# Four of eight gate/up pairs by sevens, and residual additions and wide h tiles 150 places later in the order

## The chip, the cores and the metric

One NeuronCore of a Trainium2 chip runs the whole program. The time is device microseconds of one execution; the median of 3 runs stands for the kernel. TensorE (PE) multiplies, VectorE (DVE) and ScalarE (ACT) do the elementwise work, SyncE (SP) issues the loads.

## The reference

Two decoder layers over 256 tokens of width 2048, in float32. Layer 0 mixes tokens by causal pooling over four groups, layer 1 by differential attention with ALiBi; each is followed by a SwiGLU network with 5632 hidden columns. RMSNorm stands before each part and at the end.

```python
def swiglu(h, wg, wu, wd):
    return (jax.nn.silu(h @ wg) * (h @ wu)) @ wd

for i in range(DEPTH):
    hn = rmsnorm(h, norm_mix[i])
    mix = pool_mixer(...) if i % 2 == 0 else diff_attention(...)
    h = h + mix
    h = h + swiglu(rmsnorm(h, norm_ffn[i]), w_gate[i], w_up[i], w_down[i])
return rmsnorm(h, final_norm)
```

## The kernel before

**Products in halves.** Every float32 operand is split into a rounded part `hi` and a remainder `lo`, and a product is three matmuls: hi·hi, hi·lo and lo·hi, added up in PSUM.

**A step.** `group` (L138) makes a product of the 256 tokens with 1024 weight columns, in steps of 256 rows of the weight. One step loads one megabyte into `raw` (L107, three buffers), as four blocks of 128 x 512: two row blocks times two column blocks. So a step is a product of 2 x 2 blocks, and it is made in one of two ways:

- *plain*: eight block products into four banks, 24 matmuls. DVE and ACT make `whi` and `wlo` of all four blocks (L112).
- *by sevens*: a scheme of Strassen and Winograd with seven block products, 21 matmuls, into seven banks. Three of them take the raw blocks (A11·B11, A12·B21, S4·B22), four take sums of blocks. DVE makes these sums in `tsum` (L119), and their halves go to `thi` and `tlo` (L127); `whi` and `wlo` are then made of three blocks only. The left operand needs four sums too; they are made once, when the activations are transposed (`pair`, L245, the tile `e`, L260 to L268).

`whi` and `wlo` have three buffers each, `tsum`, `thi` and `tlo` one each.

**Banks.** The eight PSUM banks are named at L135: M1, M6, M7, P5, P3, P4, M2, X = 0 to 7. Plain steps write M2, P3, P4 and X, the others M1, M2, M6, M7, P5, P3, P4. When a group is done, `combined` (L195) adds the banks up into four tiles of 512 columns: two copies on ACT and eight additions on DVE (L202 to L211). The first products of the next group are issued while this goes on, each as soon as its bank is free.

**Gate and up.** `ffn` (L443) has eleven chunks of 512 gate and 512 up columns per layer, in sections of 4, 4 and 3. Each chunk is one group of eight steps (pairs 0 to 7 of the normalised input), of which pairs 2, 4 and 6 go by sevens; in chunk 0 of layer 0 only pair 6 does. After `combined`, ACT makes silu and DVE the product with up (L463, L464), and PE transposes the result into two `h` tiles (L468). Of a section's h tiles, those at places 2, 4 and 6 are made wide (eight blocks, by `e`), since the down product takes these steps by sevens.

**Down.** After each section come two groups over its h tiles, one for each half of the 2048 columns. Their results are added to the residual `x_tok` (L487).

**Order.** The kernel is written as a program in sequence; a scheduler gives each engine a fixed order from priorities that fall in the order of writing, so that work of the next chunk moves up while an engine would wait. `tc.high_priority(-n)` lets what is written in it count as n places later.

**Other places that the change touches.** The pool stage at the start takes its banks at L335. `transposed` (L270) fills the eight `xp` tiles of the next part. In attention, `oT[h]` (L609) holds the heads' results for the output product.

Of the kernel before, what the change touches and what calls it, by code (L numbers as in the profile page):

```python
# [39 lines left out]
SEVEN = (2, 4, 6)  # L40
SEVEN_DOWN = (2, 4, 6)
SEVEN_QKV = (4, 6)
SEVEN_O = (6,)

# [8 lines left out]
def trunk_kernel(ctx, tc, x_n, gains, scale_in, final_in, subln, lam_in, band, dist,  # L53
# [31 lines left out]
    dist_sb = const.tile([P, 2 * P], F32, name="dist_sb")  # L85
    ident = const.tile([P, P], F32, name="ident")
    ones = const.tile([P, P], F32, name="ones")
    nc.vector.memset(ones, 1.0)
    make_identity(nc, ident)

# [47 lines left out]
    def group(steps, pool, by_bank=0):  # L138
# [14 lines left out]
        ps = {}  # L153
# [9 lines left out]
        def products(a, seven, w, b, parts):  # L163
            first = b not in ps
            if first:
                ps[b] = bank(b)
            for at, which, block in parts:
                hi, lo = w[which]
                if seven:
                    ah, al = a[:, 0, at], a[:, 1, at]  # L170
                else:
                    k, t = at
                    if a.shape[2] == 8:
                        slot = ((A11, A21), (A12, A22))[k][t]
                        ah, al = a[:, 0, slot], a[:, 1, slot]
                    else:
                        ah, al = (a[:, k, i, t * P:(t + 1) * P] for i in range(2))
                for x, y in ((ah, hi), (ah, lo), (al, hi)):
                    left[b] -= 1
                    nc.tensor.matmul(ps[b], x, y[:, block], start=first, stop=(left[b] == 0))  # L180
                    first = False
# [13 lines left out]
    def combined(ps, pool):  # L195
# [4 lines left out]
        m1, u2, u3, p5 = (pool.tile([P, 512], F32, name=f"c{i}") for i in ("11", "12", "21", "22"))  # L200
# [5 lines left out]
        nc.vector.tensor_tensor(u2, p5, u2, ALU.subtract)  # L206
        nc.vector.tensor_tensor(p5, p5, u3, ALU.subtract)
        nc.vector.tensor_tensor(u2, ps[P3], u2, ALU.add)
        nc.vector.tensor_tensor(u3, ps[P4], u3, ALU.add)
# [35 lines left out]
    def pair(dst, src, gains, seven):  # L245

        ps = aux((P, 2, 2, P))
# [14 lines left out]
        for i, at in ((0, slice(A21, A11 + 1)), (1, slice(A22, A12 + 1, A12 - A22))):  # L262
            nc.scalar.activation(e[:, at], ps[:, i], AF.Copy, scale=1.0 if gains is None else gains[i])
        nc.vector.tensor_tensor(e[:, S1:S3 + 1], e[:, A21:A11 + 1], e[:, A22:A21 + 1], ALU.subtract)
        nc.vector.tensor_tensor(e[:, S2], e[:, S1], e[:, A11], ALU.subtract)
        nc.vector.tensor_tensor(e[:, S4], e[:, A12], e[:, S2], ALU.add)
        nc.scalar.copy(dst[:, 0], e)
        nc.vector.tensor_tensor(dst[:, 1], e, f32(dst[:, 0]), ALU.subtract)  # L268
# [11 lines left out]
    with tc.tile_pool(name="start", bufs=1, reuse_waits="tile") as st:  # L280

        warm = tmp.tile([P, 8], F32, name="warm", bufs=1)
        nc.scalar.activation(warm[:, 0:1], ones[:, 0:1], AF.Sqrt)
# [159 lines left out]
    def ffn(layer, xq, ss, next_op, next_gain):  # L443
# [62 lines left out]
    with tc.tile_pool(name="attn", bufs=1, reuse_waits="tile") as ap_, ExitStack() as heads:  # L506
# [4 lines left out]
            small[:, a:b] for a, b in ((0, 2), (2, 4), (4, 8), (8, 10), (10, 12), (12, 13), (14, 16)))  # L511
        nc.sync.dma_start(out=subln_sb, in_=subln)
# [3 lines left out]

        nc.vector.tensor_tensor(lp, lam_sb[:, 0:2], lam_sb[:, 2:4], ALU.mult)
# [75 lines left out]
        for g in range(2):  # L593
            cs = scaled(combined(group([(xp[p], p in SEVEN_QKV, w_v[g, p]) for p in range(NP)], op_), op_), (r_col, r_col))
            for h in range(4 * g, 4 * g + 4):
# [13 lines left out]
                oT[h] = op_.tile(pair_shape(h in SEVEN_O), F32R, name=f"oT{h}")  # L609
# [99 lines left out]
```

## Time and profile before

| | |
|---|---|
| median of 3 runs | 1845.67 us (1845.63 to 1845.70) |
| the profiled execution | 1846.21 us, its span 1844.4 us |
| granted TensorE clock | 0.997 |
| gate/up chunk, from its predecessor's transposes to its own (1267.02 to 1309.80) | 42.78 us |
| whole FFN of layer 1, first gate/up section (1184 to 1351): PE, DVE, ACT busy | 167.00, 151.15, 92.34 of 167 us |
| same layer, first down section (1351 to 1435): PE, DVE, ACT busy | 84.00, 76.19, 42.72 of 84 us |

Lines of the profile are lines of the kernel; most matmuls have line 180, that of the helper in `group`, and are told apart by their tiles. PEld is the load of the stationary operand, which overlaps the matmuls. Busy times of one engine count overlapping instructions once; the mean of a group is the length of one instruction. "Idle before" is the time in which an engine stood still ahead of an instruction, with what released it.

### The profile page before, as it was taken

To read this page: it belongs to the slowest core of one execution; us is meant where nothing else is said; L and a number is where in the kernel's file an instruction comes from. 1 tells how busy PE (TensorE), PEld (TensorE's weight loads), DVE (VectorE), ACT (ScalarE), POOL (GpSimd) and SP (SyncE) were. 2 spreads that over 40 slices of the span, in tenths; PEclk is the share of its full clock that TensorE was granted. 3 is DMA by queue.
4 is the path that set the end of the run, shared out by engine and by line. 5 is a ranking of instruction groups with operands and counts; after the bars stand their busy time and mean duration, and the time that the engine had idled before them with its cause. 6 is when DMAs were issued, how large, how long until landed. Compare 5 with 4: busy or idle time off the path is not lost.

```text
span 1844.4 us, 20901 instructions
## 1 busy us (share of the span) xinstructions
PE 1829.2 (99%) x8210; PEld 1495.6 (81%) x8210; DVE 1604.2 (87%) x1662; ACT 1038.0 (56%) x1006; POOL 0.7 (0%) x6
## 2 busy tenths in 40 slices
PE   9999999999999999999999999999999999999998
PEld 6788888888888888888888888788888888888886
DVE  6889998898989899988888678998989899998986
ACT  6555555555554556665566655555555555545553
POOL 0000000000000000000000000000000000000000
PEclk9999999999999999999999999999999999999999
DMA  7555555655555555555454454555555555565552
GB/s 273 183 201 187 193 210 194 210 196 194 203 198 204 202 186 183 208 180 171 173 177 164 160 188 176 205 203 187 204 205 204 188 201 183 206 227 204 206 186 111
DMA packets 50642, 356.80 MB, mean 193 GB/s; under 512 B 6000, under 2 KB 6128, under 8 KB 8048
## 3 DMA queue, kind: packets, MB, share of 16 engines
q1 hardware_dynamic: 49824, 353.85, 54.4%
q10 hardware_dynamic: 720, 1.62, 0.2%
q8 instruction: 64, 1.05, 0.2%
q14 instruction: 34, 0.28, 0.0%
HBM read 353.36 MB, written 2.10 MB: 193 GB/s over the span
## 4 chain that ended last, share of the span: by engine, by line
PE 95%; DVE 2%; ACT 1%; issue 1%; DMA 1%; SPq 0%; DVEq 0%; ACTq 0%
PE b L180 90%; PE b L250 2%; PE b L342 1%; DVE wlo L116 1%; PE b L554 1%; PE b L345 1%; PE b L584 0%; DMA w<-pool_w 0%; DMA raw<-w_gu 0%; DVE tlo L131 0%; ACT whi L115 0%; DVE tsum L121 0%; PE b L600 0%; PE b L598 0%; PE b L599 0%
## 5 line engine op out<-in xcount | busy, mean ns | idle before, releaser
L115 ACT CAST whi<-raw 128x1536 fp32r<-128x1536 f32 (+1 forms) x330 | 585.2, 1774 | 585.4 <-PE b L180 499.6
L180 PE MATMUL b<-whi,xp 128*128 128x512 f32 x2824 | 908.8, 392 | 1.2 <-DVE c L203 1.0
L116 DVE TENSOR_TENSOR wlo<-raw,whi 128x1536 fp32r<-128x1536 f32 (+1 forms) x330 | 697.3, 2113 | 193.1 <-ACT whi L115 192.9
L180 PEld LDWEIGHTS b<-whi,xp 128*128 128x128 f32 x2824 | 528.3, 188 | 110.1 <-DVE c L203 1.5
L180 PE MATMUL b<-wlo,xp 128*128 128x512 f32 x1412 | 551.8, 391 | 1.6 <-DVE wlo L116 1.6
L180 PE MATMUL b<-whi,h 128*128 128x512 f32 x1108 | 354.5, 390 | 0.0
L180 PEld LDWEIGHTS b<-wlo,xp 128*128 128x128 f32 x1412 | 265.3, 188 | 55.5 <-DVE wlo L116 1.9
L131 DVE TENSOR_TENSOR tlo<-tsum,thi 128x2048 fp32r<-128x2048 f32 x108 | 246.7, 2285 | 3.9 <-ACT thi L130 3.9
L180 PEld LDWEIGHTS b<-whi,h 128*128 128x128 f32 x1108 | 207.5, 188 | 43.1
L180 PE MATMUL b<-wlo,h 128*128 128x512 f32 x554 | 215.8, 389 | 0.0
L130 ACT CAST thi<-tsum 128x2048 fp32r<-128x2048 f32 x108 | 206.3, 1910 | 13.7 <-DVE tsum L124 13.6
L180 PE MATMUL b<-thi,xp 128*128 128x512 f32 x608 | 211.8, 390 | 0.0
L121 DVE TENSOR_TENSOR tsum<-raw 128x1024 f32<-128x1024 f32 x108 | 131.8, 1220 | 2.3 <-DMA raw<-w_v 0.6
L180 PEld LDWEIGHTS b<-thi,xp 128*128 128x128 f32 x608 | 113.9, 188 | 24.0 <-ACT thi L130 0.9
L180 PEld LDWEIGHTS b<-wlo,h 128*128 128x128 f32 x554 | 104.0, 188 | 21.3
L180 PE MATMUL b<-tlo,xp 128*128 128x512 f32 x304 | 119.5, 393 | 0.0
L180 PE MATMUL b<-thi,h 128*128 128x512 f32 x240 | 83.7, 389 | 0.0
L124 DVE TENSOR_TENSOR tsum<-tsum,raw 128x512 f32<-128x512 f32 x108 | 74.3, 688 | 2.3
L123 DVE TENSOR_TENSOR tsum<-tsum,raw 128x512 f32<-128x512 f32 x108 | 73.9, 684 | 0.6
L180 PE MATMUL b<-whi,oT 128*128 128x512 f32 x236 | 74.4, 392 | 0.0
L180 PEld LDWEIGHTS b<-tlo,xp 128*128 128x128 f32 x304 | 57.0, 188 | 16.1 <-DVE tlo L131 4.4
L180 PEld LDWEIGHTS b<-thi,h 128*128 128x128 f32 x240 | 45.1, 188 | 9.2
(147 smaller groups left out, 1192.5 us busy)
## 6 DMA issues: line engine op xcount, KB each, us to landing
raw<-w_gu SPq DMA_DIRECT2D x176, 1024.0 KB, 4.9
raw<-w_down SPq DMA_DIRECT2D x88, 1024.0 KB, 4.8
raw<-w_qk SPq DMA_DIRECT2D x32, 1024.0 KB, 4.9
raw<-w_v SPq DMA_DIRECT2D x16, 1024.0 KB, 4.8
raw<-w_o SPq DMA_DIRECT2D x16, 1024.0 KB, 4.8
raw<-pool_w SPq DMA_DIRECT2D x2, 1024.0 KB, 13.8
x_tok<-x_n SPq DMA_DIRECT2D x2, 768.0 KB, 9.0
w<-pool_w SPq DMA_DIRECT2D x2, 512.0 KB, 6.6
```

Of the source, the lines that this page charges most:

```text
L115: nc.scalar.copy(hi[:, lo_block:], raw[:, lo_block:])
L116: nc.vector.tensor_tensor(lo[:, lo_block:], raw[:, lo_block:], f32(hi[:, lo_block:]), ALU.subtract)
L121: nc.vector.tensor_tensor(t[:, T1:T3 + 1], raw[:, B11:B22 + 1], raw[:, B12:B12 + 1].broadcast_to([P, 2, 512]), ALU.add)
L123: nc.vector.tensor_tensor(t[:, T2], t[:, T1], raw[:, B22], ALU.add)
L124: nc.vector.tensor_tensor(t[:, T4], t[:, T2], raw[:, B21], ALU.add)
L130: nc.scalar.copy(hi, t)
L131: nc.vector.tensor_tensor(lo, t, f32(hi), ALU.subtract)
L180: nc.tensor.matmul(ps[b], x, y[:, block], start=first, stop=(left[b] == 0))
L250: nc.tensor.transpose(ps[:, i, 1 - t if seven else t], src(i, t), ident)
L342: nc.tensor.matmul(yp[g][t], a[:, rows], w[:, at], start=(at == 0), stop=(at == 3))
L345: nc.tensor.matmul(yp[g][t], u, v[:, at], start=(at == 0 and j == 0), stop=(at == 3 and j == 2))
L554: nc.tensor.matmul(sc[:, :nk], qk[:, 0, c, qb * P:(qb + 1) * P], qk[:, 1, c, :nk], start=True, stop=True)
```

## The change

Pair 0 joins the pairs that go by sevens in gate/up, in all chunks except the first of each layer. The first chunk of layer 0 keeps pair 6 alone, that of layer 1 pairs 2, 4 and 6.

The order of the seven products changes: in a group's first step M1, M2, P5, M7, M6, P3, P4, in later ones M1, M2, P3, P5, M7, M6, P4. P3 and P4 become one tile of two banks, and the four results of `combined` one tile `c`, so that four of its additions become two of double width. The transposes of the h tiles go to bank X instead of taking turns in banks 0 to 3.

The additions to the residual (except in a layer's last section) become two of 1024 columns and are put back by 150 places; so are the sums and halves of the wide h tiles. To make room, `dist_sb`, `ones`, `part` and `oT[4..7]` get other places.

```diff
-SEVEN = (2, 4, 6)
+SEVEN = (0, 2, 4, 6)
+BEHIND = 150
...
+    def two_banks():
+        both = psum.tile([P, 2, 512], F32, name="b45", tag="b45")
+        return [both[:, i] for i in range(2)], both
...
+    def behind(n):
+        return tc.high_priority(-n) if n else nullcontext()
...
             if seven:
-                plan.append([(M1, [(A11, 0, B11)]), (M2, [(A12, 0, B21)]), (M6, [(S2, 1, T2)]), (M7, [(S3, 1, T3)]),
-                             (P5, [(S1, 1, T1)]), (P3, [(S4, 0, B22)]), (P4, [(A22, 1, T4)])])
+                raw = [(M1, [(A11, 0, B11)]), (M2, [(A12, 0, B21)]), (P3, [(S4, 0, B22)])]
+                summed = [(P5, [(S1, 1, T1)]), (M7, [(S3, 1, T3)]), (M6, [(S2, 1, T2)]), (P4, [(A22, 1, T4)])]
+                late = 3 if plan else 2
+                plan.append(raw[:late] + summed[:3] + raw[late:] + summed[3:])
...
-            first = b not in ps
-            if first:
+            first = b not in opened
+            opened.add(b)
+            if first and b in (P3, P4) and b not in ps:
+                (ps[P3], ps[P4]), ps["both"] = two_banks()
+            elif first and b not in ps:
                 ps[b] = bank(b)
...
-        m1, u2, u3, p5 = (pool.tile([P, 512], F32, name=f"c{i}") for i in ("11", "12", "21", "22"))
+        c = latest["c"] = pool.tile([P, 4, 512], F32, name="c")
+        m1, u2, u3, p5 = (c[:, i] for i in range(4))
...
-        nc.vector.tensor_tensor(u2, p5, u2, ALU.subtract)
-        nc.vector.tensor_tensor(p5, p5, u3, ALU.subtract)
-        nc.vector.tensor_tensor(u2, ps[P3], u2, ALU.add)
-        nc.vector.tensor_tensor(u3, ps[P4], u3, ALU.add)
+        nc.vector.tensor_tensor(c[:, 1:4:2], c[:, 3:4].broadcast_to([P, 2, 512]), c[:, 1:3], ALU.subtract)
+        nc.vector.tensor_tensor(c[:, 1:3], ps["both"], c[:, 1:3], ALU.add)
...
-        ps = aux((P, 2, 2, P))
+        ps = aux((P, 2, 2, P)) if at is None else bank(at, (P, 2, 2, P))
...
+        with behind(BEHIND if at is not None else 0):
+            nc.vector.tensor_tensor(e[:, S1:S3 + 1], e[:, A21:A11 + 1], e[:, A22:A21 + 1], ALU.subtract)
+            nc.vector.tensor_tensor(e[:, S2], e[:, S1], e[:, A11], ALU.subtract)
+            nc.vector.tensor_tensor(e[:, S4], e[:, A12], e[:, S2], ALU.add)
+            nc.scalar.copy(dst[:, 0], e)
+            nc.vector.tensor_tensor(dst[:, 1], e, f32(dst[:, 0]), ALU.subtract)
...
-                    by_seven = SEVEN[-1:] if g == 0 and layer == 0 else SEVEN
+                    by_seven = SEVEN if g else SEVEN[1:] if layer else SEVEN[-1:]
...
-                        pair(ht, lambda k, t: cs[t][1][:, (2 * i + k) * P:(2 * i + k + 1) * P], None, at in SEVEN_DOWN)
+                        pair(ht, lambda k, t: cs[t][1][:, (2 * i + k) * P:(2 * i + k + 1) * P], None, at in SEVEN_DOWN, X)
...
+                    if not last:
+                        with behind(BEHIND):
+                            for t in range(2):
+                                to = x_tok[:, t, o * 1024:(o + 1) * 1024]
+                                nc.vector.tensor_tensor(to, latest["c"][:, 2 * t:2 * t + 2].rearrange("p b n -> p (b n)"),
+                                                        to, ALU.add)
+                        continue
...
+        dist_sb = hq.tile([P, 2 * P], F32, name="dist_sb")
+        nc.sync.dma_start(out=dist_sb, in_=dist)
...
+                if h < 4:
+                    oT[h] = op_.tile(pair_shape(h in SEVEN_O), F32R, name=f"oT{h}")
+                else:
+                    oT[h] = resid.tile(pair_shape(h in SEVEN_O), F32R, name="xp", tag=f"xp{h}")
```

More of the change, by code (lines that the diff above doesn't have):

```diff
@@ L1 @@
 import math
-from contextlib import ExitStack
+from contextlib import ExitStack, nullcontext
 import concourse.bass as bass
@@ L73, in trunk_kernel @@
     turn = {"aux": 0, "of": 4}
+    latest = {}
     def bank(i, shape=(P, 512)):
         return psum.tile(list(shape), F32, name=f"b{i}", tag=f"b{i}")
+    def two_banks():
+        both = psum.tile([P, 2, 512], F32, name="b45", tag="b45")
+        return [both[:, i] for i in range(2)], both
     def aux(shape=(P, 512)):
@@ L84, in trunk_kernel @@
     gain_sb = const.tile([P, 6, NK], F32, name="gain_sb")
-    dist_sb = const.tile([P, 2 * P], F32, name="dist_sb")
     ident = const.tile([P, P], F32, name="ident")
-    ones = const.tile([P, P], F32, name="ones")
-    nc.vector.memset(ones, 1.0)
-    make_identity(nc, ident)
     x_tok = resid.tile([P, 2, D], F32, name="x_tok")
@@ L152, in group @@
                 left[b] = left.get(b, 0) + 3 * len(parts)
-        ps = {}
+        ps, opened = {}, set()
         def prepared(seven, src):
@@ L243, in split, with pair @@
         nc.vector.scalar_tensor_tensor(dst[:, 1, :], src, gain, f32(dst[:, 0, :]), ALU.mult, ALU.subtract)
-    def pair(dst, src, gains, seven):
-        ps = aux((P, 2, 2, P))
+    def pair(dst, src, gains, seven, at=None):
+        ps = aux((P, 2, 2, P)) if at is None else bank(at, (P, 2, 2, P))
         for i in range(2):
@@ L260, in pair @@
         e = tmp.tile([P, 8, P], F32, name="e", bufs=1)
[L262 to L268, printed above, removed]
+        for i, to in ((0, slice(A21, A11 + 1)), (1, slice(A22, A12 + 1, A12 - A22))):
+            nc.scalar.activation(e[:, to], ps[:, i], AF.Copy, scale=1.0 if gains is None else gains[i])
+        with behind(BEHIND if at is not None else 0):
[4 more added lines that the diff above has]
+            nc.vector.tensor_tensor(dst[:, 1], e, f32(dst[:, 0]), ALU.subtract)
     def transposed(xp, j, gain, seven=()):
@@ L280, in trunk_kernel @@
     with tc.tile_pool(name="start", bufs=1, reuse_waits="tile") as st:
+        ones = st.tile([P, P], F32, name="ones")
+        nc.vector.memset(ones, 1.0)
         warm = tmp.tile([P, 8], F32, name="warm", bufs=1)
+        make_identity(nc, ident)
         nc.scalar.activation(warm[:, 0:1], ones[:, 0:1], AF.Sqrt)
@@ L334, in product @@
             if some[0] == 0:
-                yp[g] = [bank(4 + 2 * (g % 2) + t) for t in range(2)]
+                yp[g] = [bank(6 + t) for t in range(2)] if g % 2 else two_banks()[0]
                 if g >= PLAIN:
@@ L413, in trunk_kernel @@
     turn["of"] = 4
-    nc.sync.dma_start(out=dist_sb, in_=dist)
     def finish(cs, ys, final_sb, ss):
         for t in range(2):
-            part = tmp.tile([P, 64], F32, name="part", bufs=2)
+            part = tmp.tile([P, 8], F32, name="warm", bufs=1) if t == 0 else \
+                tmp.tile([P, 2, 4], F32, name="ss").rearrange("p a b -> p (a b)")
             nc.vector.tensor_reduce(part[:, 0:1], ss[:, t, 0:2], AX.X, ALU.add)
@@ L515, in trunk_kernel @@
         nc.vector.tensor_scalar(qs_col, r_col, QK_SCALE, None, ALU.mult)
+        ones = hq.tile([P, P], F32, name="ones")
+        nc.vector.memset(ones, 1.0)
         nc.vector.tensor_tensor(lp, lam_sb[:, 0:2], lam_sb[:, 2:4], ALU.mult)
@@ L608, in trunk_kernel @@
                     nc.scalar.activation(on[:, t, :], op[:, t, :], AF.Copy, scale=ro[:, t:t + 1])
-                oT[h] = op_.tile(pair_shape(h in SEVEN_O), F32R, name=f"oT{h}")
+                if h < 4:
+                    oT[h] = op_.tile(pair_shape(h in SEVEN_O), F32R, name=f"oT{h}")
+                else:
+                    oT[h] = resid.tile(pair_shape(h in SEVEN_O), F32R, name="xp", tag=f"xp{h}")
                 pair(oT[h], lambda i, t: on[:, t, i * P:(i + 1) * P], [gs[:, i:i + 1] for i in range(2)], h in SEVEN_O)
```

## The prediction

> **What bounds the kernel now.** I read the shares and the chain of waits on the page first, then the page's waits for TensorE's weight loads.
>
> ```profile
> span 1844.4 us, 20901 instructions
> PE 1829.2 (99%) x8210; PEld 1495.6 (81%) x8210; DVE 1604.2 (87%) x1662; ACT 1038.0 (56%) x1006; POOL 0.7 (0%) x6
> PE 95%; DVE 2%; ACT 1%; issue 1%; DMA 1%; SPq 0%; DVEq 0%; ACTq 0%
> PEld b L180 <- DVE tlo L131: 6.9, 17, 0.4
> ```
>
> TensorE (PE) holds 95% of the chain that ended last and nearly all of it is line 180, the weight products. It waits for almost nothing: the longest total on its weight loads is 6.9 us for `tlo`, 17 times. So today a matmul taken out is time taken out. VectorE (DVE) at 87% is the second engine, and it is the one that this change loads. The chain in order of time (start, us, engine, line, count) gives the price of a matmul, and under it two windows of one gate/up chunk each (PE's clock, DMA share and GB/s at the end; asked for DVE alone, so the busy time is DVE's) give the state of DVE:
>
> ```profile
> 1267.02 0.66 PE b L250 x6
> 1267.68 41.44 PE b L180 x181
> 1309.80 0.65 PE b L250 x6
> 1310.45 124.34 PE b L180 x547
> ```
>
> ```profile
> 96.58:138.99 42.41, 37.70 (x34) 1.00 0.57 198
> 1267.02:1309.80 42.78, 38.90 (x37) 1.00 0.56 197
> ```
>
> A run of 547 products takes 124.34 us: 0.2273 us from one to the next (each lasts longer; they overlap). A gate/up chunk, from transposes to transposes, is 1309.80 - 1267.02 = 42.78 us. In it DVE is busy 38.90 us; in the one from 96.58, in which both h tiles made are plain, 37.70. What DVE does with the rest, from the waits of DVE in 1267 to 1309.8, and what ACT waits for in the whole run:
>
> ```profile
> DVE wlo L116 <- ACT whi L115: 3.7, 3, 1.6
> ACT whi L115 <- PE b L180: 499.6, 224, 4.7
> ```
>
> DVE's 3.7 us are waits for ACT's casts, and those wait for PE to give a weight buffer back. So DVE is idle because it is ahead, with all buffers full: a spare of 3.7 us a chunk, and 42.78 - 3.7 = 39.1 us is what its work there occupies.
>
> **The change part by part.**
>
> *Fewer products.* A plain step issues 4 banks x 2 parts x 3 = 24 matmuls, a step by sevens 7 x 3 = 21. SEVEN gains pair 0, but not in chunk 0 of either layer, so 20 of 22 chunks lose 3 matmuls: 60 x 0.2273 = **-13.6 us** on the engine that sets the end; a chunk's need of PE falls from 42.78 to 42.1. The Trainium skill, "TensorE: Matmul & The Clock Gate", section "Part 2: What happens when you issue a matmul", gives about 216 ns between matmuls of 512 columns; this trace has 227. By the page the saving would be 12.9 us, an estimate from its figure; the trace decides.
>
> *More preparation.* Each of these 20 steps gets three sums and a second pair of halves. In order of time on DVE:
>
> ```profile
> 1305.41 0.68 DVE L207 TENSOR_TENSOR c<-c,c 128x512 f32<-128x512 f32 x1
> 1306.01 0.68 DVE L208 TENSOR_TENSOR c<-b,c 128x512 f32<-128x512 f32 x1
> 1306.61 0.68 DVE L209 TENSOR_TENSOR c<-b,c 128x512 f32<-128x512 f32 x1
> 1307.21 0.68 DVE L211 TENSOR_TENSOR c<-b,c 128x512 f32<-128x512 f32 x1
> 1307.81 1.40 DVE L464 SCALAR_TENSOR_TENSOR c<-c,r_tok,c 128x512 f32<-128x512 f32 x2
> ...
> 1311.74 0.68 DVE L255 TENSOR_TENSOR h<-b,h 128x512 fp32r<-128x512 f32 x1
> ...
> 1319.65 1.75 DVE L116 TENSOR_TENSOR wlo<-raw,whi 128x1536 fp32r<-128x1536 f32 x1
> 1321.32 1.22 DVE L121 TENSOR_TENSOR tsum<-raw 128x1024 f32<-128x1024 f32 x1
> 1322.57 0.69 DVE L123 TENSOR_TENSOR tsum<-tsum,raw 128x512 f32<-128x512 f32 x1
> 1323.30 0.69 DVE L124 TENSOR_TENSOR tsum<-tsum,raw 128x512 f32<-128x512 f32 x1
> 1323.91 2.28 DVE L116 TENSOR_TENSOR wlo<-raw,whi 128x2048 fp32r<-128x2048 f32 x1
> 1326.11 2.28 DVE L131 TENSOR_TENSOR tlo<-tsum,thi 128x2048 fp32r<-128x2048 f32 x1
> 1328.43 1.23 DVE L121 TENSOR_TENSOR tsum<-raw 128x1024 f32<-128x1024 f32 x1
> ```
>
> From start to start, `wlo` of three blocks takes 1.67, the sums 1.25, 0.73 and 0.61, `tlo` 2.32: 6.58 us, at best 6.3 where nothing depends on the line before. The plain `wlo` it replaces takes 2.20. So +4.1 to +4.4; I take 4.25 a chunk, 85 us of DVE in all. What ACT adds, from the groups kept apart by shape:
>
> ```profile
> L115 ACT CAST whi<-raw 128x2048 fp32r<-128x2048 f32 x222 | 424.9, 1914 | 375.4 <-PE b L180 342.5 <-ACT h L254 18.4 <-issue 4.6
> L130 ACT CAST thi<-tsum 128x2048 fp32r<-128x2048 f32 x108 | 206.3, 1910 | 13.7 <-DVE tsum L124 13.6
> L115 ACT CAST whi<-raw 128x1536 fp32r<-128x1536 f32 x108 | 160.4, 1485 | 210.0 <-PE b L180 157.1 <-DVE c L209 33.7 <-issue 16.8
> ```
>
> One more cast of 1910 ns and one of 1485 in place of 1914: +1.5 us a chunk. ACT is 56% busy and hides it. DMA moves the same megabyte a step.
>
> The rows also show that one DVE instruction starts 0.60 us after the one before though it lasts 0.68: the ends overlap. The Trainium skill, "VectorE: DVE Perf Modes", section "Terms", says under DRAIN that the next operation cannot issue until the pipe is empty. Read as the recorded length, that would make lengths add up; the trace shows them overlapping by 0.08, so I add starts.
>
> *Merged additions.* In `combined` four DVE operations (L206 to L209) become two of 1024 elements. The nearest row is L121, 1024 elements with a broadcast: 1.13 to 1.25 apart. 4 x 0.60 = 2.40 becomes 2.3 to 2.5: between -0.1 and +0.1 a chunk; if PSUM read across two banks cost twice, +1.1. I take -0.1, as reads from PSUM (L208) and SBUF (L207) last alike. The residual additions, 4 x 0.60 merged into 2 x 1.13, likewise.
>
> *The sum on DVE.* 39.1 + 4.25 - 0.1 = 43.2 us in a chunk with one h tile by sevens, 42.0 where both are plain, against PE's 42.1: the spare of 3.7 turns into a deficit of 1.1. This is the heart of the case. What softens it: gate/up chunks come in runs of four, four and three. The first of a run has plain h tiles (no deficit); the last one's `e` work is put back by 150 places, past most of the 180 products of a chunk, so into the down projection. That work, in lengths and less 0.08 for each overlap, is 0.34 + 0.2 + 0.2 + 1.14 = 1.9 us:
>
> ```profile
> L268 DVE TENSOR_TENSOR h<-e,h 128x1024 fp32r<-128x1024 f32 x16 | 19.5, 1218 | 0.0
> L264 DVE TENSOR_TENSOR e<-e 128x256 f32<-128x256 f32 x25 | 10.4, 417 | 0.6 <-ACT e L263 0.4
> L266 DVE TENSOR_TENSOR e<-e 128x128 f32<-128x128 f32 x25 | 7.0, 282 | 0.0
> L265 DVE TENSOR_TENSOR e<-e 128x128 f32<-128x128 f32 x25 | 7.0, 280 | 0.0
> ```
>
> A run of four then wants 42.0 + 43.2 + 43.2 + 41.3 = 169.7 against 168.4, a run of three 126.5 against 126.3. It begins with DVE about 3 us ahead, and the down groups let it catch up:
>
> ```profile
> 1351.00:1393.00 42.00, 38.08 (x33) 1.00 0.56 201
> ```
>
> There DVE keeps its 3.9 us of idle, as down's sevens do not change. On average the deficit (1.3 us a run) fits into the lead, so it costs nothing by the mean.
>
> *Where it does not fit.* `tsum`, `thi` and `tlo` have one buffer each. `thi` of the next step by sevens can only be cast when the last product of the one before is done; cast 1.9 and `tlo` 2.2 make it ready 4.3 us (with the handover) later, and PE wants it after one plain step and its first raw products, 24 x 0.2273 + 6 x 0.2273 = 6.8 us. So the lead is never over 2.5 to 3 us, and at a chunk's end the same window holds `combined`. Around a boundary DVE now owes, from the end of step 6 to the first use of step 2's sums, 5.5 + 12.3 = 17.8 us: two `tlo` 4.5, `combined` 4 x 0.60 + 2 x 1.15 = 4.7, L464 1.3, L255 0.6, `wlo` 2.2 + 1.67, one set of sums 2.6: 17.6 us. That is even. A handover or two of 0.1 to 0.2 us that does not overlap is a PE stall, between 0 and 0.7 us a chunk. I take 0.2: 20 x 0.2 = **+4 us**.
>
> *Order of the banks, and the put-back.* Later sevens run nine raw products ahead of the sums instead of six, 3 x 0.23 = 0.7 us more time for `tlo`; this can end the waits shown above, each 0.4 of a weight load: bounds 0 and -6.9. I take **-1** as chunks' first step has only six. The residual additions put back (2 x 1.13 us) fall into the next stage's middle: DVE is full there in gate/up, so moving them gains at the boundary what it costs later: 0, bounds -1 and +2. If they ran too late, the cast into the single tile `c` at the next chunk's end would queue behind them on ACT and with it the following `whi` casts; 150 places are about 24 us of a 42 us chunk, so it has some 10 us left.
>
> *Elsewhere.* xp0 by sevens, once per layer, adds an `e` (1.9 us) in place of two splits, 2 x (0.48 - 0.08) = 0.8 us:
>
> ```profile
> L243 DVE SCALAR_TENSOR_TENSOR xp<-b,gain_sb,xp 128x256 fp32r<-128x256 f32 x32 | 14.4, 477 | 0.5 <-ACT xp L242 0.4
> ```
>
> Before the first chunk of layer 0 this may show, 0 to +1; I take 0.5. `dist_sb` loaded later, `ones` twice, oT in the xp buffers: none delays a reader in the rows; 0.
>
> Sum against the profiled execution's own 1846.2 (span 1844.4 and 1.8 around it; the median of the three runs is 1845.7): 1846.2 - 13.6 + 4 - 1 + 0.5 = 1836.1, and half a microsecond less on the median. I say **1836**.
>
> **The rivals.**
>
> *Wholly hidden.* The spare and the order suffice; the 60 products go and half of the `tlo` waits: 1846 - 13.6 - 2 = about 1830.5. For it: DVE's mean in the FFN stays under PE's. Against: 17.6 of 17.8 us at each boundary, with no room for a handover.
>
> *A new wait at bank X eats the gain.* All transposes of a chunk now share bank 7, one pair after the other, and step 1's last six products want it.
>
> ```profile
> 1305.53 0.39 PE L180 MATMUL b<-whi,h 128*128 128x512 f32 x1
> ...
> 1310.16 0.66 ACT L263 ACTIVATE e<-b 128x256 f32<-128x256 f32 x2 [2.10 <-PE b L250]
> ```
>
> The next group's products begin at 1305.53 and L255, the last reader of the transposes, ends at 1312.42: 6.9 us after. One pair after the other adds about 0.5 of transposes and up to 1.3 of reading (0.66 of L263, 0.68 of L255): 7.4 to 8.7. PE wants the bank after (21 + 18) x 0.2273 = 8.9 us. If DVE is 0.9 us late, 0.68 a chunk is lost, all of the saving: 1846.
>
> *DVE becomes the bound (the slower side).* In gate/up DVE's need, 43.2 us, sets the chunk if the lead is not held, from the point where its need passes 42.78, today's chunk. Then 20 x (43.2 - 42.78) = +8.4: 1854. For it: the trace's own sum exceeds PE's need; single buffers. Against: the deferred `e` and plain tiles bring a run's mean to 42.4 and down's 3.9 us lie between the runs.
>
> *Lengths add on DVE.* If each DVE instruction held up the next for its whole length, the chunk's 37 and two more would each take 0.08 us more: 43.2 + 39 x 0.08 = 46.3 a chunk, 20 x (46.3 - 42.78) = +70: 1916. The rows L207 to L211 above speak against it, each starts before the last has ended. (This is what the Trainium skill's DRAIN rule would make of the time.)
>
> **How the numbers follow.** The forecast (1832 to 1842 its own range, stalls of 0 to 0.5 us a chunk): 0.60. Wholly hidden, 1829 to 1832: 0.12. Eaten at bank X or by other waits, 1842 to 1849: 0.13. DVE bound, 1850 to 1860: 0.13. Lengths add: 0.02. About 0.2% (3.7 us) is what a measurement of this kernel can tell from no change. So faster 0.72, same 0.13, slower 0.15. The range 1830 to 1849 leaves out the last two and a little of the second.
>
> **What would show it.** Right: 60 fewer matmuls at L180; gate/up chunks of 42.1 to 42.6 us; DVE's waits for `whi` in them nearly gone; PE's weight loads waiting for `tlo` or `wlo` a few tenths a chunk, first at chunk boundaries, less in the first chunk of a run. Wrong towards slower: chunks of 43 us in a row with DVE never idle. Wrong towards bank X: PE waits that name L255 or L211 just ahead of step 1's end. If the two merged operations last over 1.3 us, my price of `combined` fails.

## The result, and the profile after

The changed kernel takes **1909.26 us** (median of 4 runs, 1907.07 to 1911.53), the kernel before 1845.68 (4 runs, 1845.63 to 1845.84). The ratio is 1.0344, 95% interval 1.0326 to 1.0362: slower by 3.4%, where 1836 was forecast. The profiled execution took 1911.5 us, its span 1909.8.

The page of the changed kernel: the span, the engines' busy time with their instructions, and the chain that ended last by engine.

```profile
span 1909.8 us, 20743 instructions
PE 1850.7 (97%) x8150; PEld 1479.4 (77%) x8150; DVE 1677.5 (88%) x1649; ACT 1055.8 (55%) x1028; POOL 0.7 (0%) x6
PE 76%; DVE 13%; ACT 4%; issue 4%; DMA 3%; SPq 0%; ACTq 0%; DVEq 0%
```

The 60 matmuls are gone (8150 in place of 8210), and still the chain holds 76% of TensorE where it held 95%. DVE took its place in the chain, with 13%, though its share of busy time hardly moved (87% to 88%). At the price that the prediction took for a product, 60 x 0.2273 = 13.6 us were saved, so 63.6 + 13.6 = **77.2 us** of waiting are new: 3.9 us for each of the 20 chunks that the change gives a fourth step by sevens.

The waits of the changed kernel (engine, line and tile that waits, what released it: total us, times, longest), and below them those of the kernel before:

```profile
ACT thi L135 <- DVE tsum L129: 193.4, 66, 5.5
DVE tlo L136 <- ACT thi L135: 79.4, 46, 2.3
PEld b L190 <- DVE tlo L136: 28.6, 40, 2.0
PEld b L190 <- ACT thi L135: 24.6, 50, 1.4
PE b L190 <- DVE tlo L136: 16.9, 18, 1.5
```

```profile
ACT thi L130 <- DVE tsum L124: 13.6, 29, 4.0
DVE tlo L131 <- ACT thi L130: 3.9, 3, 2.0
```

This is one chain, seen at each of its links: DVE makes the sums, ACT's cast waits for them (13.6 us became 193.4), DVE waits for the cast to make `tlo` (3.9 became 79.4), and TensorE waits for both halves (6.9 us before for `tlo`).

Where it happens, from windows of the changed kernel, one chunk of a section of four each (start to end; width, busy us of PE, PEld, DVE, ACT and POOL; clock, DMA share, GB/s). The marks are the starts of `combined`'s last addition, L220:

```profile
360.38:403.00 42.62, 41.09 (x178) 31.86 (x176) 37.76 (x33) 22.93 (x18) 0.00 (x0) 1.00 0.41 150
403.00:451.99 48.99, 46.32 (x199) 36.22 (x200) 46.81 (x40) 26.37 (x21) 0.00 (x0) 1.00 0.59 213
451.99:498.48 46.49, 43.39 (x183) 34.16 (x182) 41.50 (x37) 24.31 (x20) 0.00 (x0) 0.96 0.51 183
498.48:540.00 41.52, 41.52 (x189) 34.19 (x188) 37.52 (x33) 22.54 (x18) 0.00 (x0) 1.00 0.56 203
```

The first three windows are the second to fourth chunk of a section, the last one is the down group behind them, whose steps by sevens did not change; it keeps its 41.5. Against the 42.1 us that TensorE needs, the chunks lose 0.5, 6.9 and 4.4 us (the first of the section, not shown, 3.7): 15.5 in all, or 3.9 a chunk, the mean from above. The single numbers are rough, because the mark does not always fall at the same product (the first three windows hold 178, 199 and 183 instructions of TensorE, the one not shown 193); the sum over the section is not touched by that. The loss of a boundary falls just behind its mark, so into the window that begins there. DVE stands still for 2 to 5 us in each: it is not simply full.

The boundary at 403.00 in order of time, first DVE (start, us, engine, line, tile, idle before it and who ended that):

```profile
389.79 0.69 DVE L129 TENSOR_TENSOR tsum<-tsum,raw 128x512 f32<-128x512 f32 x1
392.53 2.29 DVE L136 TENSOR_TENSOR tlo<-tsum,thi 128x2048 fp32r<-128x2048 f32 x1 [2.06 <-ACT thi L135]
394.74 1.75 DVE L121 TENSOR_TENSOR wlo<-raw,whi 128x1536 fp32r<-128x1536 f32 x1
396.59 0.69 DVE L213 TENSOR_TENSOR c<-b,c 128x512 f32<-128x512 f32 x1
397.20 1.22 DVE L126 TENSOR_TENSOR tsum<-raw 128x1024 f32<-128x1024 f32 x1
398.33 0.69 DVE L214 TENSOR_TENSOR c<-b,c 128x512 f32<-128x512 f32 x1
398.94 0.68 DVE L215 TENSOR_TENSOR c<-b,c 128x512 f32<-128x512 f32 x1
399.53 0.68 DVE L128 TENSOR_TENSOR tsum<-tsum,raw 128x512 f32<-128x512 f32 x1
400.13 1.22 DVE L217 TENSOR_TENSOR c<-c 128x1024 f32<-128x1024 f32 x1
401.27 0.69 DVE L129 TENSOR_TENSOR tsum<-tsum,raw 128x512 f32<-128x512 f32 x1
401.87 1.22 DVE L218 TENSOR_TENSOR c<-b,c 128x1024 f32<-128x1024 f32 x1
403.00 0.68 DVE L220 TENSOR_TENSOR c<-b,c 128x512 f32<-128x512 f32 x1
...
404.28 2.29 DVE L136 TENSOR_TENSOR tlo<-tsum,thi 128x2048 fp32r<-128x2048 f32 x1
```

then ACT and TensorE:

```profile
392.88 1.49 ACT L120 CAST whi<-raw 128x1536 fp32r<-128x1536 f32 x1
...
402.35 1.89 ACT L135 CAST thi<-tsum 128x2048 fp32r<-128x2048 f32 x1
```

```profile
396.63 0.39 PE L190 MATMUL b<-thi,xp 128*128 128x512 f32 x1
...
403.72 0.40 PE L190 MATMUL b<-whi,xp 128*128 128x512 f32 x1
404.30 0.96 PE L190 MATMUL b<-thi,xp 128*128 128x512 f32 x3 [0.18 <-ACT thi L135]
...
406.63 0.50 PE L190 MATMUL b<-tlo,xp 128*128 128x512 f32 x1 [1.02 <-DVE tlo L136]
```

The `tlo` at 392.53 is that of step 6 of the chunk that ends. It is the last reader of `tsum`, and `tsum` has one buffer. So the sums for step 0 of the next chunk, the new ones, cannot begin before 394.82, although DVE stands idle for 2.06 us just before, and that step's weights are there by 392.88, when ACT casts them. From 394.82 on, DVE's fixed order has `wlo` and the first addition of `combined` ahead of them, so they run from 397.20 to 401.96, spread between `combined`'s additions, which free the banks. Then come the cast (402.35) and `tlo` (404.28 to 406.57). TensorE begins the last product of step 6 at 396.63. It has used up step 0's raw products by 403.95 and starts its first `tlo` product at 406.63. In the kernel before, step 0 was plain: between step 6 and step 2 there was time for the chain to go round.

### The profile page after: what moved, and what is told of

The parts are those of the page before. It is cut to its first block, busy times and chain, and to the rows that moved or that the text cites. A ratio compares the mean times of both kernels' runs of the same rounds, so it can differ in the third digit from the quotient of the medians.

```text
span 1909.8 us, 20743 instructions
## 1 busy us (share of the span) xinstructions
PE 1850.7 (97%) x8150; PEld 1479.4 (77%) x8150; DVE 1677.5 (88%) x1649; ACT 1055.8 (55%) x1028; POOL 0.7 (0%) x6
## 4 chain that ended last, share of the span: by engine, by line
PE 76%; DVE 13%; ACT 4%; issue 4%; DMA 3%; SPq 0%; ACTq 0%; DVEq 0%
PE b L190 72%; DVE wlo L121 4%; DMA raw<-w_gu 2%; ACT whi L120 2%; DVE tlo L136 2%; DVE tsum L126 1%; PE b L259 1%; DVE c L217 1%; ACT thi L135 1%; PE b L355 1%; DVE c L218 1%; DVE c L213 1%; DVE c L215 1%; DVE c L214 1%; PE b L578 1%
## 5 line engine op out<-in xcount | busy, mean ns | idle before, releaser
L190 PE MATMUL b<-whi,xp 128*128 128x512 f32 x2732 | 883.2, 393 | 9.6 <-ACT whi L120 4.3
L136 DVE TENSOR_TENSOR tlo<-tsum,thi 128x2048 fp32r<-128x2048 f32 x128 | 292.9, 2288 | 80.4 <-ACT thi L135 79.4
L135 ACT CAST thi<-tsum 128x2048 fp32r<-128x2048 f32 x128 | 244.4, 1910 | 200.1 <-DVE tsum L129 193.4
L190 PE MATMUL b<-thi,xp 128*128 128x512 f32 x784 | 270.1, 402 | 6.7 <-ACT thi L135 6.4
L190 PEld LDWEIGHTS b<-thi,xp 128*128 128x128 f32 x784 | 144.0, 189 | 51.2 <-ACT thi L135 24.6
L190 PE MATMUL b<-tlo,xp 128*128 128x512 f32 x392 | 158.0, 403 | 16.9 <-DVE tlo L136 16.9
L126 DVE TENSOR_TENSOR tsum<-raw 128x1024 f32<-128x1024 f32 x128 | 155.9, 1218 | 2.4 <-DMA raw<-w_v 1.7
L190 PEld LDWEIGHTS b<-tlo,xp 128*128 128x128 f32 x392 | 74.4, 190 | 42.8 <-DVE tlo L136 28.0
L129 DVE TENSOR_TENSOR tsum<-tsum,raw 128x512 f32<-128x512 f32 x128 | 87.7, 685 | 1.2
L128 DVE TENSOR_TENSOR tsum<-tsum,raw 128x512 f32<-128x512 f32 x128 | 87.5, 684 | 0.5
L476 ACT ACTIVATE c<-c,r_tok 128x512 f32<-128x512 f32 x44 | 31.8, 722 | 35.0 <-DVE c L214 20.8
```

The costliest lines, as they stand in the source:

```text
L126: nc.vector.tensor_tensor(t[:, T1:T3 + 1], raw[:, B11:B22 + 1], raw[:, B12:B12 + 1].broadcast_to([P, 2, 512]), ALU.add)
L128: nc.vector.tensor_tensor(t[:, T2], t[:, T1], raw[:, B22], ALU.add)
L129: nc.vector.tensor_tensor(t[:, T4], t[:, T2], raw[:, B21], ALU.add)
L135: nc.scalar.copy(hi, t)
L136: nc.vector.tensor_tensor(lo, t, f32(hi), ALU.subtract)
L476: nc.scalar.activation(gate, gate, AF.Silu, scale=r[:, t:t + 1])
```

## The experiments

The theory to which the runs led: **one buffer of `tsum`** ties step 0's sums to the end of step 6's chain and so into `combined`. It was not the first one: the expectations, written before each run, speak at first of the load of pair 0 and of the round trip through ACT (A), and later of VectorE having too much to do (A1) against a chain laid open at each boundary whatever the load (A2). That the buffer is that of `tsum` was written down only after a second buffer for `thi` had brought little. B is the put-back, C the order or bank X. The rivals: DVE is simply full (capacity); the put-back of 150 places delays what is needed; the new order of the seven products; the transposes in one bank X; the detour through ACT for the cast.

**One part taken back at a time.** First, pair 0 plain again, with all the rest of the change kept:

```diff
-                    by_seven = SEVEN if g else SEVEN[1:] if layer else SEVEN[-1:]
+                    by_seven = SEVEN[1:] if g or layer else SEVEN[-1:]
```

> The changed kernel with pair 0 plain again in every chunk; the order of the banks, the merged additions, bank X and the put-back all stay. Theory A (pair 0's preparation overloads VectorE and lays open its round trip through ScalarE; the rest of the change is about neutral): 1840 to 1850 us, within 5 us of before. Theory B (the put-back by 150 places spoils the order): still over 1880. Theory C (the single bank X or the new bank order makes the waits): still over 1870, with waits of the transposes.

Measured 1847.05 us, ratio 1.0004 (0.9994 to 1.0013). All that is slow lies in the fourth step by sevens; order, merged additions, bank X and put-back together cost nothing that can be told from zero as long as pair 0 is plain. Two of its waits belong beside those above:

```profile
ACT thi L135 <- DVE tsum L129: 86.4, 31, 4.2
DVE tlo L136 <- ACT thi L135: 48.3, 32, 2.1
```

They too are far longer than in the kernel before (13.6 and 3.9 us), and yet no time is lost, because TensorE's weight loads wait only 1.2 us for `thi` and `tlo`. The upper links of the chain can wait without harm; its last link decides.

The put-back taken out:

```diff
-BEHIND = 150
+BEHIND = 0
```

> The changed kernel with nothing put back (0 places instead of 150). Theory A: 1900 to 1925, the put-back moves VectorE work about and does not remove it. Theory B: under 1870. Theory C: as A.

1922.04 us, ratio 1.0411 (1.0390 to 1.0432): 12.8 us slower than the change. The put-back is not at fault; it helps.

The old order of the seven products:

```diff
-                raw = [(M1, [(A11, 0, B11)]), (M2, [(A12, 0, B21)]), (P3, [(S4, 0, B22)])]
-                summed = [(P5, [(S1, 1, T1)]), (M7, [(S3, 1, T3)]), (M6, [(S2, 1, T2)]), (P4, [(A22, 1, T4)])]
-                late = 3 if plan else 2
-                plan.append(raw[:late] + summed[:3] + raw[late:] + summed[3:])
+                plan.append([(M1, [(A11, 0, B11)]), (M2, [(A12, 0, B21)]), (M6, [(S2, 1, T2)]), (M7, [(S3, 1, T3)]),
+                             (P5, [(S1, 1, T1)]), (P3, [(S4, 0, B22)]), (P4, [(A22, 1, T4)])])
```

> The changed kernel with the old order of the seven products (M1, M2, M6, M7, P5, P3, P4). Theory A: the first sum is wanted 0.7 us earlier in later steps, so 1909 to 1930. Theory C, if the order is at fault: under 1880.

1908.97 us, ratio 1.0340 (1.0320 to 1.0361): no difference from the change. The order is no cause.

The two pairs of transposes in two banks:

```diff
-                        pair(ht, lambda k, t: cs[t][1][:, (2 * i + k) * P:(2 * i + k + 1) * P], None, at in SEVEN_DOWN, X)
+                        pair(ht, lambda k, t: cs[t][1][:, (2 * i + k) * P:(2 * i + k + 1) * P], None, at in SEVEN_DOWN, (X, M1)[i])
```

> The changed kernel with the second pair of transposes of each chunk in bank M1 instead of X. Theory A: the waits of the transposes on ScalarE's e and on L477 were 11 us in all, so 1898 to 1912. Theory C, if bank X is at fault: under 1880.

1914.23 us, ratio 1.0369 (1.0348 to 1.0390): 5 us slower than with one bank, and 2 us above what was expected; why was not followed up. The rival of bank X falls.

**Is DVE full?** Pair 0 by sevens only in chunks 4 and 8 of each layer, the first of a section, where the down groups before have let DVE catch up:

```diff
-                    by_seven = SEVEN if g else SEVEN[1:] if layer else SEVEN[-1:]
+                    by_seven = SEVEN if g in (4, 8) else SEVEN[1:] if g or layer else SEVEN[-1:]
```

> The changed kernel with pair 0 by sevens in chunks 4 and 8 of each layer alone, the first of a run, whose h tiles are plain (4 chunks, 12 matmuls fewer, -2.7 us). Theory A1 (the deficit builds up over a run, VectorE has too much to do): 1841 to 1847 us, the spare of the chunks around carries it. Theory A2 (at each boundary into a step by sevens the round trip from the sums through ScalarE's cast back to VectorE is laid open, whatever the load): some 3 us for each of the four, 1850 to 1860.

1858.42 us, ratio 1.0064 (1.0047 to 1.0081), that is 11.4 us over the version with pair 0 plain though it has 12 products less: (11.4 + 2.7) / 4 = 3.5 us lost for each such chunk, close to the 3.9 of the change. The window of the first of them:

```profile
307.26:352.36 45.10, 43.35 (x187) 34.34 (x185) 41.68 (x34) 22.24 (x16) 0.00 (x0) 1.00 0.60 219
```

DVE has 3.4 us of idle time in it, and the chunk before was a down group. The lead that it brings is of no use: the loss comes at a single boundary, with no run of such chunks before it.

Now DVE relieved: no wide h tiles, so the down groups are plain and their sums go.

```diff
-SEVEN_DOWN = (2, 4, 6)
+SEVEN_DOWN = ()
```

> The changed kernel with all down steps plain (30 steps, 90 matmuls more, +20.5 us in the down groups; no wide h tiles, 1.9 us less of VectorE work in 14 of the gate/up chunks). Read in its gate/up chunks: theory A1: 42.1 to 43.5 us, since need and capacity are level without e. Theory A2: still 45 or more.

In this kernel and the two that build on it `combined` does not run for the down groups, and the residual of the first two sections gets the last gate/up chunk's `c`; the down results are left out there. 1906.66 us, ratio 1.0328 (1.0308 to 1.0349).

```profile
PE 1857.1 (97%) x8240; PEld 1500.7 (79%) x8240; DVE 1493.5 (78%) x1415; ACT 989.1 (52%) x944; POOL 0.7 (0%) x6
```

DVE's share falls from 88% to 78%. The time stays, but this kernel has 90 products more than the change, 20.5 us of them: of the change's 77.2 us of waiting 54.2 are left, 2.7 a chunk. So the work taken out has a part in the loss, some 23 us, and most of the loss is there without it. A chunk of 42.1 + 2.7 = 44.8 us in the mean lies between the two theories of the expectation. The window of one of its chunks:

```profile
137.49:185.22 47.73, 45.12 (x197) 35.27 (x195) 43.40 (x37) 24.18 (x18) 0.00 (x0) 1.00 0.54 197
```

DVE is idle for 4.3 us in it, and TensorE stands still for 2.6. It waits there while DVE has time left, so capacity is not what it waits for.

**Which buffer?** The freed space takes a second buffer, of `thi` or of `tsum` (both on top of the last edit; the output tiles `y` use other tiles' space):

```diff
-        hi = pool.tile([P, 4, 512], F32R, name="thi")
+        hi = pool.tile([P, 4, 512], F32R, name="thi", bufs=2 if pool.name.startswith("ffn") else 1)
```

> As the kernel with plain down steps, and with two buffers for thi, so that the cast need not wait for the last product of the step by sevens before. Theory A1: gate/up chunks as in that kernel, within 0.3 us. Theory A2 (with the single buffer at fault): 1 to 3 us less a chunk.

1897.61 us, ratio 1.0279 (1.0259 to 1.0300): 9 us better, or 0.5 a chunk where 1 to 3 were expected of a buffer at fault. Most of the loss remains.

```diff
-        t = pool.tile([P, 4, 512], F32, name="tsum")
+        t = pool.tile([P, 4, 512], F32, name="tsum", bufs=2 if pool.name.startswith("ffn") else 1)
```

> The kernel with plain down steps (1906.7 us), with two buffers for tsum instead of one, so that the next sums can be made before tlo of the step before is done. Theory A1 (load): gate/up chunks as there, 45 to 48 us, time 1900 to 1910. Theory A2 with tsum as the buffer that binds: chunks of 42 to 44, time 1850 to 1875.

**1853.90 us**, ratio 1.0039 (1.0023 to 1.0055): 52.8 us less, by a second buffer for one intermediate tile (and another place for `y`, which is used at the very end). The same chunk:

```profile
137.30:179.10 41.80, 41.80 (x189) 34.54 (x188) 41.28 (x35) 24.44 (x18) 0.00 (x0) 1.00 0.57 202
```

TensorE is busy throughout, and the chunk takes 41.8 in place of 47.7 (of which some lies in the marks: 189 instructions of TensorE against 197). DVE is busy for 41.28 of the 41.80: nearly full, and still in time.

**Other ways to shorten the chain.** The three sums on GpSimd, which is idle:

```diff
-        nc.vector.tensor_tensor(t[:, T1:T3 + 1], raw[:, B11:B22 + 1],
+        nc.gpsimd.tensor_tensor(t[:, T1:T3 + 1], raw[:, B11:B22 + 1],
...
-        nc.vector.tensor_tensor(t[:, T2], t[:, T1], raw[:, B22], ALU.add)
-        nc.vector.tensor_tensor(t[:, T4], t[:, T2], raw[:, B21], ALU.add)
+        nc.gpsimd.tensor_tensor(t[:, T2], t[:, T1], raw[:, B22], ALU.add)
+        nc.gpsimd.tensor_tensor(t[:, T4], t[:, T2], raw[:, B21], ALU.add)
```

> The changed kernel with the three sums of the weight blocks on GpSimd instead of VectorE, in every step by sevens. It takes 2.6 us a step, 10 us a chunk, from VectorE. Theory A1: gate/up chunks fall to 42.1 us, 1832 to 1840 in all, unless GpSimd needs over 8 us for a step's sums. Theory A2: the round trip is as long or longer, so chunks stay over 44 and the time over 1880.

2198.53 us, ratio 1.1910 (1.1893 to 1.1928). The groups of that kernel (busy us, mean ns | idle before, releaser):

```profile
L126 POOL TENSOR_TENSOR tsum<-raw 128x1024 f32<-128x1024 f32 x128 | 403.0, 3149 | 1171.5 <-DVE tlo L136 667.2 <-DMA raw<-w_qk 126.6 <-DMA raw<-w_down 101.4
L128 POOL TENSOR_TENSOR tsum<-tsum,raw 128x512 f32<-128x512 f32 x128 | 320.9, 2507 | 10.0
L129 POOL TENSOR_TENSOR tsum<-tsum,raw 128x512 f32<-128x512 f32 x128 | 207.3, 1620 | 10.0
```

A set of sums takes 3.1 + 2.5 + 1.6 = 7.3 us there, against 2.6 on DVE, and GpSimd itself waits 667 us for `tlo` to give `tsum` back: it stands in the same ring and makes it longer. DVE's busy time falls by only 75 us (1602.9 of that kernel against 1677.5), since its own instructions get longer, as shown at the end, and the time rises by 289 us. Not all of it is the ring: the granted clock is 0.943 there, 0.995 in the changed kernel, and by these two up to 114 us, an estimate, would be TensorE running slower.

The cast of step 0 on DVE, without the detour through ACT:

```diff
-    def sum_halves(pool, t):
+    def sum_halves(pool, t, cast):
...
-        nc.scalar.copy(hi, t)
+        cast(hi, t)
...
-                w.append(sum_halves(pool, t))
+                w.append(sum_halves(pool, t, nc.scalar.copy if opened else nc.vector.tensor_copy))
```

> The changed kernel with the cast of thi on VectorE for the first step of each chunk (20 casts of about 1.2 us more on VectorE, no hop to ScalarE and back there). Theory A1: 1.2 us a chunk more, 1925 to 1935. Theory A2 with the hop at the boundary at fault: 0.5 to 1.5 us a chunk less, 1880 to 1900.

1944.67 us, ratio 1.0533 (1.0511 to 1.0554): 35 us slower than the change, outside of both expectations. The cast itself is shorter (1221 ns in place of 1910). But the chain got longer, not shorter. DVE at the same boundary in that kernel:

```profile
408.34 0.69 DVE L129 TENSOR_TENSOR tsum<-tsum,raw 128x512 f32<-128x512 f32 x1
...
412.00 1.22 DVE L135 CAST thi<-tsum 128x2048 fp32r<-128x2048 f32 x1
...
415.93 2.29 DVE L136 TENSOR_TENSOR tlo<-tsum,thi 128x2048 fp32r<-128x2048 f32 x1
```

From the end of the sums to the end of `tlo` are 9.2 us here (409.03 to 418.22) and 4.6 in the change (401.96 to 406.57), because DVE's order puts other work before the cast and between cast and `tlo`. So this edit is no remedy, but it does not show what the detour through ACT costs; that stays open.

**A second `tsum` in the whole computation.** The second buffer takes 8 KB a partition (4 x 512 numbers of 4 bytes). Room for it is made by one wide h tile fewer in a section, with `sq` in the space of `e` (and `y` as above):

```diff
-SEVEN_DOWN = (2, 4, 6)
+SEVEN_DOWN = (4, 6)
...
-        t = pool.tile([P, 4, 512], F32, name="tsum")
+        t = pool.tile([P, 4, 512], F32, name="tsum", bufs=2 if pool.name.startswith("ffn") else 1)
...
-        sq = tmp.tile([P, 512], F32, name="sq", bufs=1)
+        sq = tmp.tile([P, 512], F32, name="sq", tag="e", bufs=1)
```

> The changed kernel with two buffers for tsum; room is made by one wide h tile fewer (places 4 and 6 alone; 33 matmuls more, +7.5 us) and by sq in the buffer of e. Theory A2 with tsum: gate/up chunks 42 to 43 us, 1840 to 1855. Theory A1: chunks of 45 and more, 1900 to 1915.

**1839.82 us**, ratio 0.9963 (0.9949 to 0.9977): faster than both kernels, than the one before by 0.4%. Its control has the same edits but for the second buffer (and `y` in its old place):

> The control to the kernel with two tsum buffers and wide h tiles at 4 and 6: the same with one tsum buffer. If the second buffer did it: gate/up chunks of 44 to 48 us, 1895 to 1920. If the wide h tile left out (1.9 us of VectorE work in four chunks a layer) or sq's place did it: under 1850.

1911.18 us, ratio 1.0351 (1.0332 to 1.0371). The buffer is worth **71 us**. The engines' row of the control, and then of the version with two:

```profile
PE 1854.1 (97%) x8183; PEld 1486.0 (78%) x8183; DVE 1633.7 (86%) x1587; ACT 1038.5 (54%) x1007; POOL 0.7 (0%) x6
```

```profile
PE 1821.7 (99%) x8183; PEld 1489.1 (81%) x8183; DVE 1625.6 (88%) x1587; ACT 1042.7 (57%) x1007; POOL 0.7 (0%) x6
```

The same number of instructions on each engine, and DVE's busy time is the same within 0.5%. The same boundary with two buffers, DVE and then TensorE:

```profile
373.15 1.22 DVE L126 TENSOR_TENSOR tsum<-raw 128x1024 f32<-128x1024 f32 x1
374.29 2.28 DVE L136 TENSOR_TENSOR tlo<-tsum,thi 128x2048 fp32r<-128x2048 f32 x1
...
379.02 0.68 DVE L129 TENSOR_TENSOR tsum<-tsum,raw 128x512 f32<-128x512 f32 x1
...
384.75 2.29 DVE L136 TENSOR_TENSOR tlo<-tsum,thi 128x2048 fp32r<-128x2048 f32 x1
386.95 1.22 DVE L217 TENSOR_TENSOR c<-c 128x1024 f32<-128x1024 f32 x1
```

```profile
387.18 0.39 PE L190 MATMUL b<-thi,xp 128*128 128x512 f32 x1
387.41 0.39 PE L190 MATMUL b<-tlo,xp 128*128 128x512 f32 x1
```

Step 0's first sum (373.15) now starts ahead of step 6's `tlo` (374.29), and its own `tlo` (384.75) is done at 387.04, ahead of `combined`'s two wide additions. TensorE takes the first `tlo` product at 387.41 without standing still: it is in time by 0.4 us. The buffer works by the order that it allows: `tsum` is free earlier, and the order that the scheduler fixes for DVE has the sums earlier.

Two buffers for `tsum` again, the room taken from `wlo` instead (two buffers for three), with all wide h tiles kept:

```diff
-        lo = whl.tile([P, 4, 512], F32R, name="wlo")
+        lo = whl.tile([P, 4, 512], F32R, name="wlo", bufs=2)
```

> The changed kernel with two buffers for tsum and two instead of three for wlo. Theory A2 with tsum: 1835 to 1870, unless wlo's lead is what is missed then. Theory A1: 1905 or more, as less lead costs more.

1867.86 us, ratio 1.0117 (1.0096 to 1.0137). The waits name what it costs: DVE for TensorE to give a `wlo` back, which is not among the waits of the kernel before.

```profile
DVE wlo L121 <- PE b L190: 41.5, 36, 3.7
```

Another choice of wide tiles, which loses less in the last section (six h tiles, so place 6 is not in it), and the same without the put-back:

```diff
-SEVEN_DOWN = (4, 6)
+SEVEN_DOWN = (2, 4)
```

> As the kernel with two tsum buffers, with the wide h tiles at 2 and 4 instead of 4 and 6: the runs of three keep both, so 24 matmuls are lost to down instead of 33. If PE is the bound again: 9 x 0.2273 = 2 us less, 1837.8. If VectorE is: the same or more than 1839.8.

1839.18 us, ratio 0.9964 (0.9952 to 0.9977). The 2 us against places 4 and 6 cannot be told apart here (1839.2 and 1839.8).

```diff
-BEHIND = 150
+BEHIND = 0
```

> The same with nothing put back. If PE is the bound with room to spare: as with the put-back, 1837 to 1839. If VectorE's order at the boundaries still decides: 1840 to 1855.

1840.16 us, ratio 0.9966 (0.9954 to 0.9979): 1 us more than with the put-back, less than the runs of either kernel spread (1838.5 to 1841.6 with it). So with two buffers the put-back is worth nothing that shows; with one it was worth 12.8 us.

**All of them by one sum.** The products of a kernel, from its engine row, times 0.2273 us against the 8210 of before, on 1845.7 (beside these runs the kernel before took 1845.7 to 1846.3); what is left over is waiting:

| kernel | products | by the sum, us | measured, us | left over, us |
|---|---|---|---|---|
| pair 0 plain | 8210 | 1845.7 | 1847.1 | 1.4 |
| the change | 8150 | 1832.1 | 1909.3 | 77.2 |
| pair 0 in chunks 4 and 8 | 8198 | 1843.0 | 1858.4 | 15.4 |
| down plain | 8240 | 1852.5 | 1906.7 | 54.2 |
| and two `thi` | 8240 | 1852.5 | 1897.6 | 45.1 |
| and two `tsum` | 8240 | 1852.5 | 1853.9 | 1.4 |
| control, one `tsum` | 8183 | 1839.6 | 1911.2 | 71.6 |
| two `tsum`, places 4 and 6 | 8183 | 1839.6 | 1839.8 | 0.2 |
| two `tsum`, places 2 and 4 | 8174 | 1837.5 | 1839.2 | 1.7 |
| two `tsum`, two `wlo` | 8150 | 1832.1 | 1867.9 | 35.8 |

Wherever `tsum` has two buffers and `wlo` three, less than 2 us are left over; wherever pair 0 goes by sevens with one, 2.3 to 3.9 us for each chunk that it does so in (the least with a second `thi`).

## Why the prediction was wrong, by its steps

*"Fewer products"* was right in count and in price: 60 are gone, and in the kernels with two `tsum` and three `wlo` the time follows 0.2273 us a product to within 2 us.

*"More preparation"* and *"Merged additions"* were right. The two wide additions (L217 and L218 in the rows of the boundary) last 1.22 us, under the 1.3 from which the price of `combined` would have failed. DVE's busy time over the whole span grew by 1677.5 - 1604.2 = 73.3 us, and against the version with pair 0 plain (1599.9) by 77.6, not more than the 85 forecast for the new steps.

*"The sum on DVE"* forecast a lead of about 3 us that would carry a section, "so it costs nothing by the mean". By the mean it was not far off: with two `tsum`, and one wide h tile fewer in a section, DVE does it and TensorE stays the bound. But a lead can only be held in buffers, and the experiment with chunks 4 and 8 shows that the loss comes at the first boundary, where DVE has its whole lead.

***"Where it does not fit"* is the step that failed.** It named the single buffers of `tsum`, `thi` and `tlo`, and then followed `thi` alone. In its window of 17.8 us it counted "one set of sums 2.6", those of step 2, as if step 0's had been made ahead in DVE's idle time. They can't be: `tsum` is held until step 6's `tlo` has been made from it, at 394.82 in the rows, only 2 us before TensorE ends step 6. The rows at 397.20 to 401.96 show them inside the window, among `combined`'s additions. With them the step's own sum is 17.6 + 2.6 = 20.2 against 17.8: 2.4 us late at a boundary, where it said "even" and took 0.2. The window was also the wrong one. The loss does not fall at the first use of step 2's sums but at that of step 0's, 6.8 us behind the end of step 6 by the prediction's own count, and there the sums, the cast and `tlo` alone take 2.6 + 1.9 + 2.3 = 6.8 one after the other, with `combined`'s additions among them. Measured were 3.5 to 3.9 us a chunk in the mean; how they divide between this delay, the later steps and the half rate told of below was not worked out. That the buffer of `tsum` binds, far more than that of `thi`, is shown by doubling each: 52.8 us against 9. So the term of 20 x 0.2 = +4 us was 20 x 3.9 = +77.

*"Order of the banks, and the put-back"*: the order was priced at -1 and gave nothing measurable. The put-back was priced at 0 with bounds of -1 and +2; with one `tsum` it gains 12.8 us. That the wide h tiles' sums and the residual additions would else stand in the way at the boundaries is likely, but was not read from the trace. With two it is 0, as forecast. The 150 places, taken as about 24 us, are fewer in the trace: in the down groups behind 540 the residual additions come 3 to 12 us behind `combined`'s last addition (543.17 behind 540.31, 593.27 behind 581.43).

*The rivals.* Bank X fell by experiment. "DVE becomes the bound" was the nearest, with the side right, but by the wrong mechanism: it named 43.2 us of work a chunk as the limit and 1854 as the time. The chunks took up to 49 us with DVE idle for 2 to 5 us, and with 11% of DVE's load taken away 54 of the 77 us were still lost. "Lengths add" is out too: starts 0.60 apart with lengths of 0.68 stand in the rows above as they did before.

What stays open: a version with two `tsum`, three `wlo` and all wide h tiles, which would want 1832 by the sum, was not run; nor was one with a single `tsum` and the sums put ahead of `wlo` and `combined`'s additions, which would tell how much of the 77 us a better order alone wins back. Open are also the cost of the detour through ACT, and why a second `thi` alone brings 9 us, though the sums stay tied to `tsum`.

## What to carry to other kernels

An engine's idle share is a reserve only if the work can be done early, and that needs a free buffer for its result: for each added step, walk the ring of its intermediates (who writes, who reads last, when the buffer is free) and put that time, not the mean of busy shares, against the time the consumer leaves. A chain from DVE to ACT and back to DVE with one buffer at its head can begin its next turn only when the last reader has given that buffer back, whatever the engines' shares. When the list of waits shows the same chain growing at all its links, down to the engine that sets the end, as `tsum` to `thi` to `tlo` to TensorE here, try doubling the buffer at its head first: here both ways of moving a link to another engine lost time. The upper links alone are no sign: with pair 0 plain they waited 86 and 48 us at no loss.

## What the hardware showed beside that

Waits of TensorE can cost more than their length. After 489 us in the changed kernel (TensorE in order of time):

```profile
486.64 1.19 PE L190 MATMUL b<-thi,xp 128*128 128x512 f32 x4 [0.46 <-ACT thi L135]
489.36 0.54 PE L190 MATMUL b<-tlo,xp 128*128 128x512 f32 x1 [1.52 <-DVE tlo L136]
489.70 0.63 PE L190 MATMUL b<-thi,xp 128*128 128x512 f32 x1
...
493.11 0.39 PE L190 MATMUL b<-wlo,xp 128*128 128x512 f32 x1
```

Behind two waits of 0.46 and 1.52 us, eight matmuls stand 0.43 us apart instead of 0.23, from 489.70 to 493.11: 3.41 us at half rate, 1.6 us lost on top of the waits. The granted clock in the window around it is 0.96, and over the whole span 0.995 where it was 0.997 before; by those two, an estimate, it is some 4 us of the 77. The Trainium skill, "TensorE: Matmul & The Clock Gate", section "Part 1: The HAM clock gate (the "warmup" mystery)", tells of windows of 3413 ns after which the rate changes, and of half rate after an idle one. The length agrees with the 3.41 us here; but TensorE was not idle for a whole window, it had run four products between the two waits.

GpSimd is slower than its idle share promises, and DVE and GpSimd slow each other. Beside the groups shown above, of the kernel with the sums on GpSimd:

```profile
L121 DVE TENSOR_TENSOR wlo<-raw,whi 128x2048 fp32r<-128x2048 f32 x202 | 538.7, 2667 | 144.8 <-ACT whi L120 144.5
```

`wlo` of 2048 elements takes 2667 ns in the mean there, and 2.29 us in the rows of the other kernels. `tlo`, of the same size, keeps 2288 ns in that kernel: it is made while GpSimd waits for it, and none of the 128 overlaps an addition on GpSimd. The other way round, the additions of 512 elements at L128 take 1.28 us on GpSimd where no addition, subtraction or product on DVE overlaps them (11 of 128) and 2.6 us in the mean where one does. An addition of 1024 elements takes 3149 ns on GpSimd, such overlaps included, and 1.22 us on DVE.
